# Attention: key tiles of row pitch 128, small tiles moved, so that all matmul operands share one byte residue modulo 256

## The chip, the core and the metric

The kernel runs on one NeuronCore of a Trainium2 chip. TensorE (PE in the profile) does the matrix products and the transposes; VectorE (DVE), ScalarE (ACT) and GpSimd (POOL) do the elementwise work; SyncE (SP) issues most DMAs. The metric is device time in microseconds (us) of one execution; the times given are medians of several runs.

In a matmul here the *stationary* operand is a 128x128 tile that is first loaded into the array (PEld in the profile), and the *moving* operand streams through it, 128x512 in most products of this kernel. Both lie in SBUF, 128 partitions with a line of bytes each; the result goes to PSUM. Where a tile begins in its line is decided by the order and the sizes in which pools and tiles are allocated. "Byte residue" below is that start address modulo 256.

## The reference, cut to what matters

One encoder layer over 2048 positions of width 1024: a projection, a gated linear attention (group A), a latent attention (group B), an output projection and a layer norm. The change lies in group B, a dense softmax attention with 4 heads over all 2048 keys:

```python
def attend(blk):
    qn, qr = blk
    s = (jnp.einsum('bqhd,bkhd->bhqk', qn, k_nope, preferred_element_type=jnp.float32)
         + jnp.einsum('bqhr,bkr->bhqk', qr, k_r, preferred_element_type=jnp.float32))
    p = jax.nn.softmax(s, axis=-1)
    return jnp.einsum('bhqk,bkhv->bqhv', p.astype(v.dtype), v)
...
x = layer_norm(DEEPNORM_ALPHA * x + mixed, ln_g[layer], ln_b[layer])
```

The kernel absorbs the up-projections into the queries and the output, so that all four heads share one key of width 128 (`ckvT`), one rotary key (`krs`) and one value (`vh`, `vl`).

## The kernel before

Every fp32 value that enters a matmul is split into a high part (rounded to fp32r, by ACT) and a low part (the rest, by DVE or POOL). A product is then three matmuls: high x high, high x low, low x high (`mm3`, lines 420 to 422).

The program has four stages. `sweep_a` (to about 380 us) projects x for group A, with weights `wah`, `wal` and products `ipa`; the gate's products `ipg` have the moving operand `wgh`/`wgl`, 512 wide, and the stationary `xah`/`xal`. `sweep_c` projects x for group B and fills the key and value tiles (`c_ckvTh`, `c_ckvTl`, `c_krT`, `vh`, `vl`), one row of 128 floats for each of 16 chunks of 128 positions. `attention` follows, and an output projection closes, with products `po`, `pmb`, `px` (moving `woh`/`wol`, 512 wide; stationary `oh`/`ol`); its first products run inside the last block of attention.

`attention` runs 16 blocks (4 heads x 4 groups of 512 queries). A block has 8 units of two key tiles. For each key tile `scores` issues five matmuls (lines 1521 to 1525) with a row of `ckvT_h`, `ckvT_l` or `krs` stationary and a query tile `qh`, `ql`, `rh`, `rl` moving, all 512 wide, into the PSUM tile `pS`. ACT copies `pS` to `s` (L1530), DVE keeps a running maximum `rm` (L1543). After the 8 units `tmax` transposes `rm` on PE (`mx`, L1549), `rmax` reduces it to a column `mc` (L1554), `bmax` transposes it back (`mb`, L1561). DVE subtracts (L1567), ACT takes the exponential (L1571), ACT and POOL split it into `ph` and `pl` (L366, L372), and `pv` multiplies: `ph` or `pl` moving, a row of `vh` or `vl` stationary, six matmuls for each unit, into `o`. The sums go through `tsum` (`sx`, L1630) to a column `rc` (`rcp`); `turn` and `rows` do that for the last block, with a row tile `rr` that is named `rt`. `y` is three more matmuls, with `ofh`, `ofl` moving.

A table of places (`PLACE` and its like) sorts all these steps into one order, and each engine runs its instructions in that order. So the scores of one block alternate with the value products of the block before.

The pools: `wz` holds the query tiles (and later `oh`, `ol`), `sp` the scores `s`, `bp` the tiles `ph`, `pl`, `ofh`, `ofl`, `wv_h`, `wv_l`, and, between them, the columns `mc` and `rc` and the row tile of `rows`. `smo` (of `OutProj`) holds small tiles of the output stage. `res`, on the right side, holds the three key tiles with `KW` = 132 floats (528 bytes) for a row of 128, and the two value tiles with 128. A tile `edge` of 32 bytes on the right side is never read or written.

Of the kernel before, what the change touches and what calls it, by code (L numbers as in the profile page):

```python
# [9 lines left out]
F32 = mybir.dt.float32  # L10
F32R = mybir.dt.float32r
# [7 lines left out]
P = 128  # L19
# [8 lines left out]
QB = 512  # L28
NQB = S // QB
NKT = S // P  # L30
KW = P + 4
TAU_INV = 1.0 / 16.0
RMS_EPS = 1e-6
LN_EPS = 1e-5
# [106 lines left out]
    tm=(0.532, 1.152),  # L141
# [79 lines left out]
    tm=(0.445, 1.143),  # L221
# [65 lines left out]
    tm=(0.495, 1.083),  # L287
# [68 lines left out]
class K:  # L356
# [141 lines left out]
    def run(self):  # L498
        tc, nc, ins = self.tc, self.nc, self.ins
        with ExitStack() as top:  # L500
            cp = top.enter_context(tc.tile_pool(name="const", bufs=1))
            self.cp = cp
            dp = top.enter_context(tc.tile_pool(name="scr", bufs=1, space=DRAM))
            self.qd_s = [dp.tile([P, H * P], F32, name=f"qd_s{c}") for c in range(NCH)]
            self.oi_s = [dp.tile([P, H * P], F32, name=f"oi_s{c}") for c in range(NCH)]
            self.su_s = [dp.tile([P, H * P], F32, name=f"su_s{c}") for c in range(NCH)]
            self.u_s = [dp.tile([P, H * P], F32, name=f"u_s{c}") for c in range(NCH)]
            self.qa_s = [[dp.tile([P, H, QB], F32, name=f"q{p}_s{b}") for p in "hl"] for b in range(NQB)]
            self.qr_s = [[dp.tile([H, 64, QB], F32, name=f"r{p}_s{b}") for p in "hl"] for b in range(NQB)]
            self.gm_s = [dp.tile([P, H, QB], F32, name=f"gm_s{b}") for b in range(NQB)]  # L510
            self.oa_s = [dp.tile([P, H, P], F32, name=f"oa_s{c}") for c in range(NCH)]
            self.r_s = [dp.tile([1, H, QB], F32, name=f"r_s{b}") for b in range(NQB)]
            self.ob_s = [dp.tile([P, H, QB], F32, name=f"ob_s{b}") for b in range(NQB)]

            ident = cp.tile([P, P], F32, name="ident")
            self.ident = ident
            self.gkv_c = cp.tile([P, 1], F32, name="gkv_c")
            self.gn_c = cp.tile([P, 1], F32, name="gn_c")
            self.cw = cp.tile([P, NCH, 3, H], F32, name="cw")

            psum = ExitStack()
            pspool = lambda n: psum.enter_context(tc.tile_pool(name=n, bufs=2, space=PSUM, reuse_waits="tile"))
            self.gp, self.ip, self.tr = pspool("gp"), pspool("ip"), pspool("tr")
            self.xfp = top.enter_context(tc.tile_pool(name="xfp", bufs=2, reuse_waits="tile"))
            edge = top.enter_context(tc.tile_pool(name="edge", bufs=1, side="right"))
            edge.tile([P, 8], F32, name="edge")
            self.keep = top.enter_context(tc.tile_pool(name="keep", bufs=1, side="right", reuse_waits="tile"))
            wgs = ExitStack()
            self.wgp = wgs.enter_context(tc.tile_pool(name="wgp", bufs=2 * NK + 1, side="right", reuse_waits="tile"))
            self.xab = wgs.enter_context(tc.tile_pool(name="xab", bufs=2, side="right"))  # L530
            self.wgate = []
            self.wl = None
            self.sweep_a()
            self.wz = top.enter_context(tc.tile_pool(name="wz", bufs=2 * NK + 1, reuse_waits="tile"))
            bcs = ExitStack()
            self.wm = bcs.enter_context(tc.tile_pool(name="wm", bufs=2 * NK + 1, reuse_waits="tile"))
            self.bc = bcs.enter_context(tc.tile_pool(name="bc", bufs=1, reuse_waits="tile"))
            self.wl = bcs.enter_context(tc.tile_pool(name="wl", bufs=2, reuse_waits="tile"))
            self.late_gates()
            wgs.close()  # L540
            rp = top.enter_context(tc.tile_pool(name="res", bufs=1, side="right", reuse_waits="tile"))
            self.ckvT_h = rp.tile([P, NKT, KW], F32R, name="ckvT_h")
            self.ckvT_l = rp.tile([P, NKT, KW], F32R, name="ckvT_l")
            self.kr = rp.tile([P, NKT, KW], F32R, name="krs")
            self.vh = rp.tile([P, NKT, P], F32R, name="vh")
            self.vl = rp.tile([P, NKT, P], F32R, name="vl")
            self.sweep_c()
            bcs.close()
            psum.close()
            self.wof = top.enter_context(tc.tile_pool(name="wof", bufs=PRE_W, side="right", reuse_waits="tile"))  # L550
            self.attention()
# [59 lines left out]
    def sweep_a(self):  # L611
        tc, nc, ins, cp = self.tc, self.nc, self.ins, self.cp
        with ExitStack() as ctx:
# [94 lines left out]
            for i in range(4, NCH):  # L708
# [12 lines left out]
                if i == 9:  # L721
                    self.rope_tables(hpi)
            i = NCH - 1
            run("q", i)
            run("k", i)
            run("av", i - 1)
# [598 lines left out]
        self.lo(s["cqT_l"][:, :, j], d["tm"][:, 0:2], s["cqT_h"][:, :, j])  # L1325

    def c_ckvTh(self, d):
        self.hi(self.ckvT_h[:, d["c"], :P], d["tm"][:, 2])

    def c_ckvTl(self, d):  # L1330
        self.lo(self.ckvT_l[:, d["c"], :P], d["tm"][:, 2], self.ckvT_h[:, d["c"], :P])

    def c_krT(self, d):
        self.hi(self.kr[:, d["c"], :P], d["tm"][:, 3])


    def c_pqr(self, d):
# [149 lines left out]
    def attention(self):  # L1487
# [4 lines left out]
        with ExitStack() as ctx:  # L1492
            qp = self.wz
            sp = ctx.enter_context(tc.tile_pool(name="sp", bufs=NP + 4, reuse_waits="tile"))
            bp = ctx.enter_context(tc.tile_pool(name="bp", bufs=2, reuse_waits="tile"))
# [17 lines left out]
            def scores(i, j):  # L1513


                d = stt[i]
                qh, ql, rh, rl = d["q"]
                ps = d["ps", j] = pS.tile([P, 2, QB], F32, tag="pS", name=f"pS{i}_{j}")
                for e in range(2):
                    kh, kl, kr = (t[:, 2 * j + e, :P] for t in (self.ckvT_h, self.ckvT_l, self.kr))  # L1520
                    mm(ps[:, e], kh, qh, start=True, stop=False)  # L1521
                    mm(ps[:, e], kh, ql, start=False, stop=False)  # L1522
                    mm(ps[:, e], kl, qh, start=False, stop=False)  # L1523
                    mm(ps[:, e], kr, rh, start=False, stop=False)  # L1524
                    mm(ps[:, e], kr, rl, start=False, stop=True)  # L1525
# [24 lines left out]

            def rmax(i):
                d = stt[i]
                d["mc"] = bp.tile([P, 4], F32, tag="mc", name=f"mc{i}")
                V.tensor_reduce(d["mc"], d["x"], AX.X, ALU.max)  # L1554

            def bmax(i):
# [75 lines left out]
            def rcp(i):  # L1632

                d = stt[i]
                rc = bp.tile([P, 4], F32, tag="rc", name=f"rc{i}")
                V.tensor_reduce(rc, d["x"], AX.X, ALU.add)
                V.reciprocal(rc, rc)
                d["rc"] = rc
# [11 lines left out]

            def rows(i):
                h, b = blocks[i]
                rr = bp.tile([4, P], F32, tag="rm", name=f"rt{i}", bufs=1)
                Ac.activation(rr, stt[i]["rt"], AF.Copy)
                nc.sync.dma_start(self.r_s[b][:, h].rearrange("o (e p) -> (o e) p", p=P), rr)

# [32 lines left out]
            op = OutProj(self, ctx, qp, bp, sp, pS, pM, pX, pO, pA)  # L1689
# [14 lines left out]
            for i in range(nb):  # L1704
                for j in range(NP):
                    t = NP * i + j
                    put(t, scores, i, j)
                    for n, f in (("copy", copy), ("max", smax), ("sub", sub), ("exp", exp), ("hi", phi), ("lo", plo),
                                 ("pv", pv), ("acc", acc)):
                        if n != "acc" or j != SUM_POOL[0] or i == nb - 1:  # L1710
                            put(t + at(n, i, j), f, i, j)
                put(NP * i + at("acc0", i), acc0, i)
                for n, f in (("tmax", tmax), ("rmax", rmax), ("bmax", bmax)) + {nb - 1: (), nb - 2: own_late}.get(i, own):
                    put(NP * i + NP - 1 + at(n, i), f, i)
                if i + 2 < nb:
                    put(NP * i + 4.05, fetch, i + 2)
# [70 lines left out]
            for c in range(4, NCH):  # L1787
                with fixed():
                    split(c + 2)
                    load(c + 4)  # L1790
                    if 4 < c < NCH - 1:
                        op.load_res(rest[c + 1])
                    op.product(rest[c])
                    op.finish(rest[c])
                with self.after(*last.values()), fixed():
                    if c == 4:
                        keep(nb - 2)
                    for f in {4: (tot, oh, ol), 5: (tsum, rcp), 7: (turn, y, rows, yc)}.get(c, ()):
                        f(nb - 1)
# [212 lines left out]
```

## Time and profile before

| | |
|---|---|
| median of 3 runs | 1317.59 us (1316.13 to 1318.52) |
| profiled execution: span, first to last instruction | 1311.9 us |
| PE busy in it | 1288.3 us, 98% |
| DVE / ACT / POOL busy | 958.5 / 812.5 / 784.6 us |
| granted TensorE clock | 0.998 of full |

The profile gives the span of its execution, not that execution's time as the runs are timed; the median lies 5.7 us above the span, which is what lies around the first and the last instruction. A sum that is made on the trace is made against 1311.9 us and carried to 1317.59 us. Durations of matmuls in the profile overlap: a matmul is shown for some 395 ns while the next starts some 230 ns after it. What a matmul costs is the distance from its start to the next one's start, which the timeline view gives to 10 ns.

### The profile page before, as it was taken

The page shows a single profiled execution, that of the slowest core. Times are in us where ns is not written, and L with a number is a line of the kernel's source. Part 1 is how long each engine was busy: PE and PEld are TensorE (multiplying, and loading weights), DVE is VectorE, ACT ScalarE, POOL GpSimd, SP SyncE. Part 2 cuts the span into 40 slices and gives each one's busy share as a digit, 9 for nine tenths or more (in the row PEclk, how much of TensorE's full clock was granted, in tenths as well). Part 3 has the DMA queues.
Part 4 walks back from the last instruction along what each step waited for, and adds up shares of the span by engine and source line. Part 5 has one row for each costly group of instructions (what it writes and reads, how often), then busy time and mean ns, then how long its engine had stood idle before and what let it go on. Part 6 is the DMA issues. An engine that isn't in the chain of part 4 may idle for free.

```text
span 1311.9 us, 19981 instructions
## 1 busy us (share of the span) xinstructions
PE 1288.3 (98%) x7081; PEld 1129.9 (86%) x7081; DVE 958.5 (73%) x1712; ACT 812.5 (62%) x1339; POOL 784.6 (60%) x494
## 2 busy tenths in 40 slices
PE   7999999999999999999999999999999999999997
PEld 7999999999989999999788888888888887888786
DVE  7967684655675455554888888888888888468998
ACT  6765656555575656564687787888888888511110
POOL 0143333232457666671388888889999999844441
PEclk9999999999999999999999999999999999999999
DMA  8131313122475555565301111112223210366663
GB/s 283 61 100 53 93 53 92 49 76 71 147 245 173 197 194 177 201 202 177 121 1 41 41 42 41 41 57 59 63 66 102 51 41 9 121 208 174 210 195 121
DMA packets 107819, 145.81 MB, mean 111 GB/s; under 512 B 17250, under 2 KB 62694, under 8 KB 107720
## 3 DMA queue, kind: packets, MB, share of 16 engines
q1 hardware_dynamic: 99128, 142.41, 35.0%
q0 software_dynamic: 672, 2.10, 0.4%
q8 instruction: 56, 0.92, 0.3%
q10 hardware_dynamic: 7920, 0.03, 0.3%
q14 instruction: 43, 0.35, 0.2%
HBM read 94.14 MB, written 50.36 MB: 110 GB/s over the span
## 4 chain that ended last, share of the span: by engine, by line
PE 83%; DVE 4%; DMA 3%; ACT 2%; issue 2%; POOL 1%; SPq 1%; DVEq 0%; POOLq 0%; ACTq 0%
PE o L420 4%; PE o L421 4%; PE pS L1521 4%; PE pS L1524 4%; PE o L422 4%; PE pS L1523 4%; PE pS L1525 4%; PE pS L1522 4%; PE ipa L420 4%; PE ipa L422 4%; PE ipa L421 4%; PE pz L421 2%; PE pz L420 2%; PE pz L422 2%; PE ipg L420 2%; PE ipg L421 2%
## 5 line engine op out<-in xcount | busy, mean ns | idle before, releaser
L372 POOL TENSOR_TENSOR pl<-s,ph 128x1024 fp32r<-128x1024 f32 x128 | 306.9, 2412 | 66.7 <-ACT ph L366 61.5
L1543 DVE TENSOR_TENSOR rm<-pS,rm 128x512 f32<-128x512 f32 x210 | 144.8, 690 | 44.1 <-ACT s L1530 39.0
L1530 ACT ACTIVATE s<-pS 128x1024 f32<-128x1024 f32 x128 | 131.2, 1025 | 67.6 <-PE pS L1525 65.6
L1567 DVE TENSOR_TENSOR s<-s,mb 128x1024 f32<-128x1024 f32 x128 | 151.2, 1213 | 9.5 <-PE mb L1561 9.3
L1030 POOL TENSOR_TENSOR Us<-Us,cw 128x512 f32<-128x512 f32 x16 | 18.5, 1157 | 227.0 <-DVE Us L1028 175.2
L366 ACT ACTIVATE ph<-s 128x1024 fp32r<-128x1024 f32 x128 | 135.0, 1057 | 18.1 <-PE o L422 17.6
L1571 ACT ACTIVATE s<-s 128x1024 f32<-128x1024 f32 x128 | 131.4, 1050 | 13.8 <-DVE s L1567 13.7
L420 PE MATMUL ipa<-wah,xah 128*128 128x384 f32 (+1 forms) x384 | 130.6, 340 | 6.8 <-ACT wah L366 6.8
L422 PE MATMUL ipa<-wah,xal 128*128 128x384 f32 (+1 forms) x384 | 125.2, 326 | 0.0
L421 PE MATMUL ipa<-wal,xah 128*128 128x384 f32 (+1 forms) x384 | 125.0, 325 | 0.0
L1521 PE MATMUL pS<-qh,ckvT_h 128*128 128x512 f32 x256 | 103.7, 405 | 0.7 <-ACT s L1571 0.4
L420 PE MATMUL o<-ph,vh 128*128 128x512 f32 x256 | 102.6, 401 | 0.0
L422 PE MATMUL o<-ph,vl 128*128 128x512 f32 x256 | 101.3, 396 | 0.0
L1524 PE MATMUL pS<-rh,krs 128*128 128x512 f32 x256 | 101.2, 395 | 0.0
L421 PE MATMUL o<-pl,vh 128*128 128x512 f32 x256 | 101.1, 395 | 0.0
L1523 PE MATMUL pS<-qh,ckvT_l 128*128 128x512 f32 x256 | 100.9, 394 | 0.0
L1525 PE MATMUL pS<-rl,krs 128*128 128x512 f32 x256 | 100.7, 393 | 0.0
L1522 PE MATMUL pS<-ql,ckvT_h 128*128 128x512 f32 x256 | 100.6, 393 | 0.0
L1594 DVE TENSOR_TENSOR ap<-ap,s 128x512 f32<-128x512 f32 x120 | 83.1, 693 | 2.7 <-ACT s L1571 0.8
L372 POOL TENSOR_TENSOR ol<-of,oh 128x512 fp32r<-128x512 f32 x32 | 43.0, 1346 | 65.6 <-ACT oh L366 65.6
L420 PEld LDWEIGHTS ipa<-wah,xah 128*128 128x128 f32 x384 | 73.5, 192 | 7.6 <-ACT wah L366 6.8
L420 PE MATMUL pz<-xch,wzh 128*128 128x256 f32 x256 | 74.8, 292 | 0.0
(325 smaller groups left out, 3856.4 us busy)
## 6 DMA issues: line engine op xcount, KB each, us to landing
xcf<-xT_dram SPq DMA_DIRECT2D x16, 512.0 KB, 4.7
xr<-x_dram SPq DMA_DIRECT2D x16, 512.0 KB, 6.5
out_dram<-rr SPq DMA_DIRECT2D x32, 256.0 KB, 2.0
xaf<-xT_dram SPq DMA_DIRECT2D x14, 512.0 KB, 4.2
oib<-oi_s SPq DMA_DIRECT2D x16, 256.0 KB, 4.1
qdb<-qd_s SPq DMA_DIRECT2D x16, 256.0 KB, 4.6
SU<-su_s SPq DMA_DIRECT2D x16, 256.0 KB, 4.4
ub<-u_s SPq DMA_DIRECT2D x16, 256.0 KB, 4.7
```

What stands on the lines that cost most here:

```text
L366: return nc.scalar.activation(dst, src, AF.Copy).ins
L372: return e.tensor_tensor(dst, src, hi.bitcast(F32), ALU.subtract).ins
L420: mm(out, ah, bh, start=start, stop=False)
L421: mm(out, ah, bl, start=False, stop=False)
L422: mm(out, al, bh, start=False, stop=stop)
L1521: mm(ps[:, e], kh, qh, start=True, stop=False)
L1522: mm(ps[:, e], kh, ql, start=False, stop=False)
L1523: mm(ps[:, e], kl, qh, start=False, stop=False)
L1524: mm(ps[:, e], kr, rh, start=False, stop=False)
L1525: mm(ps[:, e], kr, rl, start=False, stop=True)
L1543: V.tensor_tensor(d["rm"], src[:, e], d["rm"], ALU.max)
L1567: V.tensor_tensor(s, s, d["mb"][:, None, :].to_broadcast([P, 2, QB]), ALU.subtract)
```

## The change

The key tiles get a row pitch of 128 floats (512 bytes), like the value tiles, and the columns `mc` and `rc` and the row tile `rr` move from the pool `bp` to `smo`. No arithmetic changes.

```diff
-KW = P + 4
...
-            self.ckvT_h = rp.tile([P, NKT, KW], F32R, name="ckvT_h")
-            self.ckvT_l = rp.tile([P, NKT, KW], F32R, name="ckvT_l")
-            self.kr = rp.tile([P, NKT, KW], F32R, name="krs")
+            self.ckvT_h = rp.tile([P, NKT, P], F32R, name="ckvT_h")
+            self.ckvT_l = rp.tile([P, NKT, P], F32R, name="ckvT_l")
+            self.kr = rp.tile([P, NKT, P], F32R, name="krs")
...
-        self.hi(self.ckvT_h[:, d["c"], :P], d["tm"][:, 2])
+        self.hi(self.ckvT_h[:, d["c"]], d["tm"][:, 2])
...
-                    kh, kl, kr = (t[:, 2 * j + e, :P] for t in (self.ckvT_h, self.ckvT_l, self.kr))
+                    kh, kl, kr = (t[:, 2 * j + e] for t in (self.ckvT_h, self.ckvT_l, self.kr))
...
-                d["mc"] = bp.tile([P, 4], F32, tag="mc", name=f"mc{i}")
+                d["mc"] = op.sm.tile([P, 4], F32, tag="mc", name=f"mc{i}")
...
-                rc = bp.tile([P, 4], F32, tag="rc", name=f"rc{i}")
+                rc = op.sm.tile([P, 4], F32, tag="rc", name=f"rc{i}")
...
-                rr = bp.tile([4, P], F32, tag="rm", name=f"rt{i}", bufs=1)
+                rr = op.sm.tile([4, P], F32, tag="rm", name=f"rt{i}", bufs=1)
```

What that does to the places, from the addresses in the two built programs (bytes modulo 256, of every tile or row that stands):

| operand | role | before | with the change |
|---|---|---|---|
| `qh`, `ql`, `rh`, `rl` | moving, scores | 192 | 192 |
| rows of `ckvT_h`, `ckvT_l`, `krs`, key tile kt | stationary, scores | 192 + 16 kt, modulo 256 | 192 |
| `ph`, `pl` | moving, products with the values | 0 | 192 |
| rows of `vh`, `vl` | stationary | 192 | 192 |
| `ofh` / `ofl` | moving, `y` | 0 / 192 | 192 / 192 |
| `wv_h`, `wv_l` | stationary, `y` | 192 | 192 |
| `ident` | moving, transposes | 128 | 128 |
| `wgh`, `wgl` and `xah`, `xal` | gate in `sweep_a` | 192 and 192 | 192 and 192 |
| `woh`, `wol` and `oh`, `ol` | output projection | 192 and 192 | 192 and 192 |
| `wmh`, `wml` and `xch`, `xcl` | `ipm` in `sweep_c`, 448 wide | 192 and 192 | 192 and 192 |

The order of the instructions is the same on all five engines. What moves is one group of waits. `mc` now lies where an `oT` tile of `sweep_c` lay, so the first `mc` must wait for the DMAs that stored it; before, the first `rc` lay there and waited. On DVE, at the first maximum of attention (`rm` running maximum, `mx` the transposed maximum in PSUM), before:

```order
L1543 TENSOR_TENSOR rm_7865<-s_6_7952,rm_7865 128x512 [waits DVE_49]
L1543 TENSOR_TENSOR rm_7865<-s_7_7967,rm_7865 128x512 [waits DVE_49,Activation_49]
L1543 TENSOR_TENSOR rm_7865<-s_7_7967,rm_7865 128x512 [waits DVE_49]
L1554 TENSOR_REDUCE mc_7987<-mx_7982 128x4 [waits PE_49]
L1540 TENSOR_TENSOR rm_8007<-pS_0_7969,s_0_7994 128x512 [waits DVE_49,Activation_49]
L1567 TENSOR_TENSOR s_2_7882<-s_2_7882,mb_7989 128x1024 [waits PE_49]
```

and with the change:

```order
L1542 TENSOR_TENSOR rm_7865<-s_6_7952,rm_7865 128x512 [waits DVE_49]
L1542 TENSOR_TENSOR rm_7865<-s_7_7967,rm_7865 128x512 [waits DVE_49,Activation_49]
L1542 TENSOR_TENSOR rm_7865<-s_7_7967,rm_7865 128x512 [waits DVE_49]
L1553 TENSOR_REDUCE mc_7987<-mx_7982 128x4 [waits DMAHW5_49,DMAHW3_49,DMAHW7_49,DMAHW1_49,PE_49]
L1539 TENSOR_TENSOR rm_8007<-pS_0_7969,s_0_7994 128x512 [waits DVE_49,Activation_49]
L1566 TENSOR_TENSOR s_2_7882<-s_2_7882,mb_7989 128x1024 [waits PE_49]
```

The four DMA waits stand ahead of the first `mc`, and in exchange the first `rc`, a block later, waits for PE alone. Every line number above 31 is one lower.

More of the change, by code (lines that the diff above doesn't have):

```diff
@@ L1327, in c_ckvTh @@
     def c_ckvTh(self, d):
-        self.hi(self.ckvT_h[:, d["c"], :P], d["tm"][:, 2])
+        self.hi(self.ckvT_h[:, d["c"]], d["tm"][:, 2])
     def c_ckvTl(self, d):
-        self.lo(self.ckvT_l[:, d["c"], :P], d["tm"][:, 2], self.ckvT_h[:, d["c"], :P])
+        self.lo(self.ckvT_l[:, d["c"]], d["tm"][:, 2], self.ckvT_h[:, d["c"]])
     def c_krT(self, d):
-        self.hi(self.kr[:, d["c"], :P], d["tm"][:, 3])
+        self.hi(self.kr[:, d["c"]], d["tm"][:, 3])
     def c_pqr(self, d):
```

## The prediction

> **What bounds the kernel now.** I read the chain of waits first, then the busy times by stage, then PE's timeline, start by start.
>
> ```profile
> PE 83%; DVE 4%; DMA 3%; ACT 2%; issue 2%; POOL 1%; SPq 1%; DVEq 0%; POOLq 0%; ACTq 0%
> 0.00:616.40 616.40, 603.98 (x4000) 571.88 (x4001) 382.05 (x901) 373.05 (x830) 267.95 (x248) 1.00 0.44 138
> 616.40:1159.40 543.00, 540.56 (x2427) 438.61 (x2426) 441.41 (x589) 418.00 (x450) 453.12 (x198) 1.00 0.21 59
> 1159.40:1311.90 152.50, 143.78 (x658) 119.39 (x657) 135.02 (x224) 21.47 (x59) 63.49 (x48) 0.98 0.60 189
> 794.03 0.44 PE mb L1561 x4
> 825.77 0.44 PE mb L1561 x4
> 857.51 0.44 PE mb L1561 x4
> ...
> 1107.91 0.63 PE mx L1549 x4
> ...
> 1151.38 3.44 DMA xr<-x_dram
> ```
>
> The first row is the chain's shares by engine. In the next three each engine has its busy time and its count: PE, PEld, DVE, ACT, POOL; the second of them is attention, where PE is busy 540.56 of 543.00 us. The rest are pieces of the chain. The three `mb`, one for each block, have PE work alone between them, 31.74 us apart both times; the last block's maximum follows at 1107.91, and at 1151.38 the chain leaves PE for a load. So in attention a block lasts as long as PE's matmuls need, and the question is what one costs.
>
> ```profile
> 792.04 0.60 PE L1549 MATMUL mx<-ident,rm 128*128 128x128 f32 x4
> 792.40 0.48 PE L420 MATMUL o<-ph,vh 128*128 128x512 f32 x1
> 792.72 0.40 PE L421 MATMUL o<-pl,vh 128*128 128x512 f32 x1
> ```
>
> Four transposes take 0.36 us to the next start, and the 512-wide matmul behind them 0.32. A block has three such sets (`mx`, `mb`, `sx`), 2.04 us, and 128 other 512-wide matmuls (80 scores, 48 with the values, 3 of `y`, less the three just counted). They get (31.74 - 2.04)/128 = 232.0 ns each. The clock is 1.00 here, so it isn't the throttle.
>
> **The same shape elsewhere is cheaper.** The output projection streams 128x512 too:
>
> ```profile
> 1192.36 0.60 PE L1630 MATMUL sx<-ident,acc 128*128 128x128 f32 x4
> 1192.71 0.48 PE L420 MATMUL pmb<-woh,oh 128*128 128x512 f32 x1
> 1193.03 0.40 PE L421 MATMUL pmb<-wol,oh 128*128 128x512 f32 x1
> 1194.19 0.40 PE L420 MATMUL pmb<-woh,oh 128*128 128x512 f32 x1
> 1195.57 0.39 PE L420 MATMUL pmb<-woh,oh 128*128 128x512 f32 x1
> 1214.38 0.39 PE L422 MATMUL po<-woh,ol 128*128 128x512 f32 x1
> 1195.57:1214.38 18.81, 18.81 (x84) 15.58 (x83) 12.11 (x21) 2.19 (x5) 10.15 (x8) 1.00 0.63 169
> ```
>
> From 1195.57 to 1214.38 there are 84 starts, 83 distances: 226.6 ns. Right behind the transposes it is slower: 5 distances from 1193.03 to 1194.19 (232 ns), 11 to 1195.57 (230.9). So a stream whose operands all have residue 192 settles at 226.6 within eleven matmuls of a disturbance, which costs 11 x 4.3 = 47 ns, or 5 x 5.4 = 27 if it is cut off after five.
>
> Is it the residue, or is it that ACT has little to do there? Two stretches tell these apart.
>
> ```profile
> 79.74 0.39 PE L420 MATMUL ipg<-wgh,xah 128*128 128x512 f32 x1
> 84.27 0.39 PE L422 MATMUL ipg<-wgh,xal 128*128 128x512 f32 x1
> 79.74:84.27 4.53, 4.53 (x21) 3.75 (x20) 4.17 (x4) 0.61 (x2) 3.23 (x2) 1.00 0.14 33
> 1133.49 0.40 PE L420 MATMUL po<-woh,oh 128*128 128x512 f32 x1
> 1136.26 0.40 PE L420 MATMUL o<-ph,vh 128*128 128x512 f32 x1
> 789.72 0.39 PE L1521 MATMUL pS<-qh,ckvT_h 128*128 128x512 f32 x1
> 790.87 0.40 PE L1521 MATMUL pS<-qh,ckvT_h 128*128 128x512 f32 x1
> ```
>
> The gate's products in `sweep_a`, residue 192 throughout, take 4.53/20 = 226.5 ns with DVE and POOL busy. The output projection's own products, put in twelves between products with `ph` and `pl` (residue 0) in the last block, take 2.77/12 = 230.8. So the price follows the operands and what ran just before, not the stage. The last two rows are the case against: the five scores of key tile 0 have residue 192 on both sides already, and take 1.15/5 = 230 ns. I read them as the eleven-long settling seen above, cut off after five; but it is a reading.
>
> **The change part by part.**
>
> *Scores and value products.* All 131 matmuls of a block come to residue 192 on both sides. Of a steady block: three sets 2.04, 128 x 226.6 = 29.00, settling 27 ns behind `mx` (its six matmuls end in `mb`) and 47 behind `mb` and `sx`, 0.12. Sum 31.16, so 0.58 us less. Blocks 2 to 14 are thirteen of them: 7.5 us. The last block's part to 1107 us has the same matmuls: 0.55. From there to the end of its products at 1159 the mix of `o` and `po` runs at 230.8 or less, some with its settling already in it: of the 170 or so to 1151, where DMAs and DVE take the chain over, at most 0.7; I take 0.5.
>
> ```profile
> 616.40:635.10 18.70, 18.70 (x84) 15.17 (x83) 11.25 (x16) 9.73 (x11) 1.30 (x1) 1.00 0.82 261
> 635.10:662.70 27.60, 25.79 (x113) 20.10 (x112) 23.77 (x31) 22.11 (x24) 16.23 (x7) 1.00 0.10 29
> ```
>
> Block 0 is 80 scores with PE full: 80 x 5.4 less one settling, 0.4. In block 1 PE idles 1.8 us for DVE and ACT, so its gain is between nothing and 0.5; I take 0.1, since what waits ends on the others. Sum: 7.5 + 0.55 + 0.5 + 0.4 + 0.1 = 9.05 us.
>
> Bounds: at best no settling is lost and all of blocks 1 and 15 counts, 13 x 128 x 5.4 = 9.0, and 0.7 + 0.7 + 0.43 + 0.5: 11.3 us. At least, if the stream settles only half of the time between its disturbances, half of 9.05: 4.5 us.
>
> The Trainium skill speaks against any gain: on the page "TensorE: Matmul & The Clock Gate", section "Step-by-step: what each phase is for", it says that loading the next tile's weights "doesn't steal SBUF read bandwidth from the running matmul", the two having ports of their own. By it an address can't matter, and the time stays. The 226.6, 230.8 and 232.0 ns of one shape at one clock don't fit it.
>
> *Do the others follow?* A block 0.58 us shorter needs data 0.58 us sooner.
>
> ```profile
> 792.68 0.69 DVE L1554 TENSOR_REDUCE mc<-mx 128x4 f32<-128x512 f32 x1 [0.96 <-PE mx L1549]
> 793.87 0.60 PE L1561 MATMUL mb<-ident,mc 128*128 128x128 f32 x4
> 1043.60:1075.40 31.80, 31.80 (x145) 25.84 (x144) 27.06 (x37) 26.41 (x30) 31.27 (x16) 1.00 0.17 41
> 1045.58 7.14 POOL L372 TENSOR_TENSOR pl<-s,ph 128x1024 fp32r<-128x1024 f32 x3
> 1055.90 0.40 PE L421 MATMUL o<-pl,vh 128*128 128x512 f32 x1
> ```
>
> The tightest hand-over of a steady block is `mc`: it ends at 793.37, 0.50 us ahead of the transposes that read it, and only six matmuls (0.03 us of gain) lie between the maximum's transposes and these. POOL is the engine to watch: in block 14 it works 31.27 us, more than the 31.16 that the block would last. But the third `pl` of the group ends at 1052.72, 3.18 us before PE takes it, so POOL may fall behind by 0.1 to 0.5 us in each of three blocks without a wait.
>
> *The moved wait.*
>
> ```profile
> 618.14 0.58 SPq L1458 DMA_DIRECT2D oa_s<-oT  x1
> DMA to landing us min/median/max: 2.0/4.0/10.1
> 638.50 0.69 DVE L1554 TENSOR_REDUCE mc<-mx 128x4 f32<-128x512 f32 x1 [0.75 <-PE mx L1549]
> ```
>
> The last store of an `oT` is issued at 618.14 and the slowest of them lands after 10.1 us, so by 628.3; the first `mc` starts at 638.50. Behind it on DVE stand block 1's maximum and the subtractions, which PE waits for; with ten us of cover the price is nothing, and it would be the lateness of the store otherwise. The other small tiles move without a wait. `ph` and `pl` are written at another residue by ACT and POOL; POOL's `pl` takes 7.14/3 = 2.38 us at residue 0, and I expect the same.
>
> The output stage has the operands that it had. It starts 9 us sooner and lasts as long.
>
> **Rivals.** *The residue does nothing* (attention's own traffic makes the 232). For it: key tile 0. Against: `po` at 230.8 and 226.6. Time 1317.6. It is what the skill's rule above would give.
>
> *Slower: a shared residue settles at a dearer distance.* A stream need not settle low:
>
> ```profile
> 463.12 0.37 PE L422 MATMUL ipm<-wmh,xcl 128*128 128x448 f32 x1
> 466.22 0.36 PE L422 MATMUL ipm<-wmh,xcl 128*128 128x448 f32 x1
> ```
>
> These 448-wide products have residue 192 everywhere and stand at 3.10/15 = 206.7 ns, 0.461 ns a column. At that rate a 512-wide one takes 236.2, 4.2 more than now: 4.2 x 128 x 15 = 8.1 us, 1325.7. It decides from 232.0 on. Against it: width and pitch of the changed operands are those of the output projection, not of `ipm`.
>
> *POOL becomes the bound* from block 13 on: the gain there (three blocks, 1.7 us) is lost, and as much again if the output stage's splits, which POOL makes in the same blocks, come late: 9.05 - 3.4 = 5.7, 1311.9. Against it stand the 3.18 us above.
>
> **How the numbers follow.** Forecast 0.80, time 1317.59 - 9.05 = 1308.5 us. POOL 0.06, no effect 0.09, slower 0.05. A measurement of this kernel tells some 0.2% from no change, 2.6 us: forecast and POOL are faster (0.86), no effect is the same (0.09), the rest slower (0.05). The range goes from the upper bound, 1317.6 - 11.3 = 1306.3, to the lower, 1317.6 - 4.5 = 1313.1, and holds the POOL case; it leaves out the 0.14 of the last two and little more.
>
> **What would show it.** The block's period between two `mb` in the chain: 31.16, not 31.74. PE's starts in a long run of scores and value products: 226 to 227 ns from the twelfth behind a set of transposes, about 231 before it. PE busy without a gap in blocks 2 to 14. The stage before 616 us unchanged, and the output stage as long as now. It would be wrong if the period stays at 31.74 (residue without effect), if it shrinks but gaps with a POOL or DVE releaser appear, or if the scores settle while the value products do not (then a score or a value product has another cause, and only one of 80 to 48 parts of the gain comes).

## The result, and the profile after

| | time, median us (lowest to highest) | ratio to before, 95% interval |
|---|---|---|
| before | 1316.86 (1314.53 to 1318.52), 6 runs | |
| with the change | 1307.47 (1306.02 to 1310.94), 6 runs | 0.9937 (0.9926 to 0.9947) |
| both once more, on another occasion | 1315.19 and 1305.86 | 0.9933 (0.9921 to 0.9946) |

The forecast was 1308.5 us with a range from 1306.3 to 1313.1. The profiled execution of the changed kernel took 1308.66 us by its own time, with a span of 1306.3: some 2.4 us lie around a span, not the 5.7 that the part on the time before supposed. The profiled execution of before was thus one of its shorter ones. The sum of the prediction is not touched by it, since it is a difference. The two medians of six runs lie 9.4 us apart, and the ratio of 0.9937 stands for 8.3 us; the forecast was 9.05.

The chain's shares by engine, then three windows of the changed kernel: up to attention, attention to its last product with the values, and the rest. The columns are those shown of before.

```profile
PE 83%; DMA 4%; DVE 3%; ACT 2%; POOL 1%; issue 1%; SPq 1%; DVEq 0%; POOLq 0%; ACTq 0%
```

```profile
0.00:616.55 616.55, 605.06 (x4000) 572.77 (x4001) 381.89 (x901) 373.34 (x830) 267.96 (x248) 1.00 0.44 138
616.55:1150.00 533.45, 530.54 (x2427) 437.60 (x2426) 441.19 (x589) 417.87 (x450) 452.26 (x198) 1.00 0.22 60
1150.00:1306.30 156.30, 145.31 (x658) 120.51 (x656) 135.17 (x224) 21.59 (x59) 63.41 (x48) 0.97 0.60 185
```

The first stage is as long as before (616.55 against 616.40 us). Attention has the same 2427 matmuls and lasts 533.45 instead of 543.00 us: the whole gain is there. The output stage lasts 156.30 instead of 152.50 us, and its granted clock is 0.97 instead of 0.98: 3.8 us are given back there in this execution.

PE's timeline in block 6, start by start:

```profile
791.04 0.60 PE L1560 MATMUL mb<-ident,mc 128*128 128x128 f32 x4
791.40 0.48 PE L1520 MATMUL pS<-qh,ckvT_h 128*128 128x512 f32 x1
791.71 0.40 PE L1521 MATMUL pS<-ql,ckvT_h 128*128 128x512 f32 x1
793.80 0.39 PE L419 MATMUL o<-ph,vh 128*128 128x512 f32 x1
801.28 0.39 PE L1520 MATMUL pS<-qh,ckvT_h 128*128 128x512 f32 x1
822.16 0.60 PE L1560 MATMUL mb<-ident,mc 128*128 128x128 f32 x4
853.25 0.60 PE L1560 MATMUL mb<-ident,mc 128*128 128x128 f32 x4
```

From one `mb` to the next it is 31.12 and 31.09 us (31.74 before). Behind the transposes the stream is still unsettled: nine distances from 791.71 to 793.80, 232 ns each. From 793.80 to 801.28, through value products and scores alike, 33 distances take 226.7 ns each. Settled runs of both kinds have one price, and it is that of the output projection.

What is new stands in the output stage:

```profile
1185.22 14.26 DMA gr<-gm_s
1199.50 0.92 SPq L1853
1200.46 7.79 DMA xr<-x_dram
1208.38 0.70 DVE rr L1926
```

```profile
1205.67 0.40 PE L421 MATMUL y<-ofh,wv_l 128*128 128x512 f32 x1
1209.22 0.47 PE L419 MATMUL pmb<-woh,oh 128*128 128x512 f32 x1 [3.15 <-DVE rr L1926]
1209.82 0.63 PE L421 MATMUL pmb<-woh,ol 128*128 128x512 f32 x1
1212.81 0.53 PE L419 MATMUL pmb<-woh,oh 128*128 128x512 f32 x1
```

```profile
1209.80:1213.00 3.20, 3.20 (x9) 2.50 (x8) 3.10 (x7) 0.92 (x3) 0.39 (x1) 0.50 0.76 235
```

The first fence is from the chain, the second from PE's timeline, the third a window. Behind the last `y` PE stands still: DVE's residual `rr` waits for the load `xr`, which SP issues at 1200.46, behind four loads of `of` and `gr`. From `y` to the next start it is 3.55 us; before, at the same place, it is 1.34:

```profile
1215.17 0.40 PE L422 MATMUL y<-ofh,wv_l 128*128 128x512 f32 x1
1216.51 0.47 PE L420 MATMUL pmb<-woh,oh 128*128 128x512 f32 x1 [0.94 <-DVE rr L1927]
```

In the changed kernel's window behind that stall the granted clock is 0.50, and the seven distances from 1209.82 to 1212.81 are 427 ns each, 200 more than those of the matmuls that follow: 1.4 us.

### The profile page after: what moved, and what is told of

Read it like the earlier page. It is cut to its first block, busy times and chain, and to the rows that moved or that the text cites. A ratio compares the mean times of both kernels' runs of the same rounds, so it can differ in the third digit from the quotient of the medians.

```text
span 1306.3 us, 19979 instructions
## 1 busy us (share of the span) xinstructions
PE 1280.9 (98%) x7081; PEld 1130.9 (87%) x7081; DVE 958.2 (73%) x1712; ACT 812.8 (62%) x1339; POOL 783.6 (60%) x494
## 4 chain that ended last, share of the span: by engine, by line
PE 83%; DMA 4%; DVE 3%; ACT 2%; POOL 1%; issue 1%; SPq 1%; DVEq 0%; POOLq 0%; ACTq 0%
PE pS L1520 4%; PE o L419 4%; PE o L420 4%; PE o L421 4%; PE pS L1522 4%; PE pS L1523 4%; PE pS L1521 4%; PE pS L1524 4%; PE ipa L419 4%; PE ipa L421 4%; PE ipa L420 4%; PE pz L420 2%; PE pz L419 2%; PE pz L421 2%; PE ipg L419 2%; PE ipg L420 2%
## 5 line engine op out<-in xcount | busy, mean ns | idle before, releaser
L1529 ACT ACTIVATE s<-pS 128x1024 f32<-128x1024 f32 x128 | 131.4, 1027 | 60.6 <-PE pS L1524 51.3
```

## The experiments

The first ones test what sets the price of a matmul: its own two operands, or the run in which it stands; and whether equal residues are needed or a regular pitch is enough.

**One half of the change each.** The key tiles alone:

```diff
-KW = P + 4
+KW = P
```

> The kernel before with the key tiles at a pitch of 128 floats, so that all scores have residue 192 on both sides; mc, rc and rr stay in bp, so that ph and pl stay at residue 0. Theory (a stream settles at 226.6 ns only when a long run of it has one residue, and any matmul of two residues unsettles it): scores run in tens between six value products, so neither settles in a steady block. Scores stay at 230 to 231 ns, value products at 232, the period at 31.6 to 31.7 us (31.74 before, 31.10 with the whole change), and the time falls by 0 to 2 us, ratio 0.9985 to 1.000. Block 0, which has scores alone, does settle: 226 to 227 ns. Rival (each matmul's price is set by its own two residues): the 80 scores of a block take 226.6 each, the value products 232: period 31.74 - 80 x 0.0054 = 31.3 us, time 6 us less, ratio 0.995.

and on the kernel before, the small tiles alone:

```diff
-                d["mc"] = bp.tile([P, 4], F32, tag="mc", name=f"mc{i}")
+                d["mc"] = op.sm.tile([P, 4], F32, tag="mc", name=f"mc{i}")
...
-                rc = bp.tile([P, 4], F32, tag="rc", name=f"rc{i}")
+                rc = op.sm.tile([P, 4], F32, tag="rc", name=f"rc{i}")
...
-                rr = bp.tile([4, P], F32, tag="rm", name=f"rt{i}", bufs=1)
+                rr = op.sm.tile([4, P], F32, tag="rm", name=f"rt{i}", bufs=1)
```

> The kernel before with mc, rc and rr in smo, so that ph and pl come to residue 192 like vh and vl; the key tiles keep the pitch of 132 floats. Theory (one residue over a long run): value products run in sixes between scores of unequal residues and do not settle: 231 ns or more, the scores 232, the period 31.6 to 31.74 us, ratio 0.9985 to 1.000. Block 0 as before, 232 ns. Rival (each matmul by its own residues): 48 value products of a block at 226.6: period 31.74 - 48 x 0.0054 = 31.48 us, time 3.9 us less, ratio 0.997. The two halves then add up to the whole; by the theory they do not.

Measured: keys alone 1311.67 us, ratio 0.9976 (0.9965 to 0.9987); small tiles alone 1311.39, ratio 0.9969 (0.9958 to 0.9980). The means are over all 512-wide matmuls of blocks 2 to 13, without the one right behind a set of transposes:

| | period, us | scores, ns | value products, ns |
|---|---|---|---|
| before | 31.74 | 232.1 | 232.5 |
| keys alone | 31.50 | 229.9 | 230.6 |
| small tiles alone | 31.51 | 231.6 | 228.7 |
| both | 31.10 | 227.3 | 227.3 |

On the period both expectations miss. The halves bring 0.24 and 0.23 us of a period, the whole 0.64: they do not add up, so the price is not set by a matmul's own operands (that rule gave 31.3 for the keys). But they bring more than the theory left them (0 to 0.1). PE's timeline of the keys alone shows why:

```profile
799.10 0.40 PE L420 MATMUL o<-ph,vh 128*128 128x512 f32 x1
801.87 0.40 PE L1521 MATMUL pS<-qh,ckvT_h 128*128 128x512 f32 x1
804.19 0.60 PE L1630 MATMUL sx<-ident,acc 128*128 128x128 f32 x4
805.77 0.39 PE L1521 MATMUL pS<-qh,ckvT_h 128*128 128x512 f32 x1
806.91 0.40 PE L420 MATMUL o<-ph,vh 128*128 128x512 f32 x1
```

Ten scores, all of residue 192 on both sides, that follow twelve value products of two residues take 2.32 us, 232 ns each; the five from 805.77, which follow other scores, take 1.13 to 1.14 us, 227 each. And the twelve value products from 799.10 to 801.87, whose operands are as before, take 230 to 231 (before, the mean of all was 232.5). So a matmul's price depends on what ran before it, as the theory says; a stream with two kinds of operands settles in parts of each run, which the theory had denied.

On block 0, which has scores alone, both expectations hold. With the keys alone, from the eighth score on:

```profile
617.94 0.39 PE L1523 MATMUL pS<-qh,ckvT_l 128*128 128x512 f32 x1
631.99 0.39 PE L1525 MATMUL pS<-rl,krs 128*128 128x512 f32 x1
```

These are 62 distances of 226.6 ns. With the small tiles alone, where the scores keep their unequal residues, the distances of block 0, all but the first, lie between 225 and 238 ns, 232 in the mean, as before.

**A constant difference.** In the changed kernel the key and value tiles are moved as a whole, pitch and order kept:

```diff
+            rp.tile([P, 16], F32, name="pad1")
             self.ckvT_h = rp.tile([P, NKT, P], F32R, name="ckvT_h")
...
             self.vl = rp.tile([P, NKT, P], F32R, name="vl")
+            rp.tile([P, 48], F32, name="pad2")
```

> The changed kernel with the key and value tiles moved by 64 bytes as a whole: stationary operands at residue 0 in every score and value product, moving ones at 192. The pitch is regular, the small tiles are moved, but the two residues differ, always by the same amount. Theory (the two residues must be equal): scores and value products do not settle, 231 to 233 ns, period 31.6 to 31.8 us, ratio 0.998 to 1.000. Rival (one regular pitch, the same address pattern from matmul to matmul, is what counts, or the moved small tiles): 226 to 227 ns, period 31.1 us, ratio 0.994 as with the change. The output projection, which is not touched, stays at 226.6 ns in either case.

Three more of the kind, with 32 and 32 floats, 8 and 56, 64 and 64:

> The changed kernel with the key and value tiles moved by 128 bytes: stationary operands at residue 64, moving ones at 192, in all scores and value products. Theory (equal modulo 256 is needed): a uniform stream settles at the price seen with 64 bytes between them, 233.3 ns, period 31.87 us. Rival (equal modulo 128 is enough): 226.7 ns and 31.10 us, as with the change.

> The changed kernel with the key and value tiles moved by 32 bytes: stationary operands at residue 224, moving ones at 192. Theory (the two must be equal to the byte): 233.3 ns, period 31.87 us. Rival (only the line of 64 bytes in which both lie counts, 192 to 255): 226.7 ns, 31.10 us.

> The changed kernel with the key and value tiles moved by 256 bytes: residues equal modulo 256, not modulo 512 (in the changed kernel they are equal modulo 512 as well). Theory (modulo 256, as the change has it): 226.7 ns, period 31.10 us. Rival (equal modulo 512 is needed): 233 ns, 31.85 us, as with 32, 64 and 128 bytes between them.

| stationary ahead of moving by | period, us | mean of 512-wide, ns | time, us |
|---|---|---|---|
| 0 (the change) | 31.10 | 227.3 | 1307.47 |
| 32 bytes | 31.85 | 233.1 | 1317.33, one run |
| 64 bytes | 31.86 | 233.2 | 1316.94, ratio 1.0016 (1.0007 to 1.0024) |
| 128 bytes | 31.84 | 233.1 | 1318.07, one run |
| 256 bytes | 31.13 | 227.5 | 1306.91, one run |

PE's timelines: 64 bytes ahead, then 32, then 256, each with the first and the last start of a run of scores and value products that no transposes break:

```profile
809.65 0.39 PE L419 MATMUL o<-ph,vh 128*128 128x512 f32 x1
817.82 0.39 PE L1524 MATMUL pS<-qh,ckvT_l 128*128 128x512 f32 x1
```

```profile
809.04 0.40 PE L1522 MATMUL pS<-qh,ckvT_h 128*128 128x512 f32 x1
817.67 0.40 PE L1522 MATMUL pS<-qh,ckvT_h 128*128 128x512 f32 x1
```

```profile
808.29 0.39 PE L419 MATMUL o<-ph,vh 128*128 128x512 f32 x1
814.41 0.39 PE L1522 MATMUL pS<-qh,ckvT_h 128*128 128x512 f32 x1
```

The runs are 35, 37 and 27 distances long: 233.4, 233.2 and 226.7 ns. So a regular pitch is worth nothing without equal residues. The first expectation had such a stream not settle, at 231 to 233 ns; it does settle, but at a dearer distance, a little above the mixture of before (232.2 ns), and with 64 bytes the kernel is slower than before with an interval above 1. A difference of 32 bytes, with both operands in the same stretch of 64, is enough to lose the gain, and so is one of 128; one of 256 loses nothing. So for these products the change's "modulo 256" is borne out from both sides. What was moved here, the key and value tiles, is read by PE alone during attention, which points to PE's own reads. The moved small tiles are in all these kernels: where they lie is no cause of its own.

**Another common residue.** All that is allocated after `sweep_a` is shifted, so that scores, value products and output projection have residue 0 on both sides:

```diff
+            top.enter_context(tc.tile_pool(name="shift", bufs=1)).tile([P, 16], F32, name="pad1")
             self.wz = top.enter_context(tc.tile_pool(name="wz", bufs=2 * NK + 1, reuse_waits="tile"))
...
             self.vl = rp.tile([P, NKT, P], F32R, name="vl")
+            rp.tile([P, 48], F32, name="pad2")
```

> The changed kernel with everything that is allocated after sweep_a moved by 64 bytes or as much modulo 256 on both sides: queries, ph, pl, keys, values, weights of the output projection all at residue 0. Theory (what counts is that the two residues are equal): 226.7 ns, period 31.10 us, output projection 226.6 ns as now. Rival (residue 192 itself is the good one): 232 to 233.3 ns, period 31.7 to 31.9 us, output projection slower too.

```profile
806.79 0.39 PE L419 MATMUL o<-ph,vh 128*128 128x512 f32 x1
816.54 0.39 PE L1522 MATMUL pS<-qh,ckvT_h 128*128 128x512 f32 x1
```

43 distances of 226.7 ns, period 31.17 us, 1307.90 us in one run; the output projection stands at 226.7. The 0.07 us by which the period exceeds the change's lie in the settling (mean of all 227.8 ns, not 227.3). Equality counts, not the value 192.

**The transposes.** `ident` at 192:

```diff
+            cp.tile([P, 16], F32, name="pad1")
             ident = cp.tile([P, P], F32, name="ident")
+            cp.tile([P, 48], F32, name="pad2")
```

> The changed kernel with ident at residue 192 in place of 128, so that the transposes too have one residue (mx and sx on both sides; mb has it in the first of its four columns). Theory (a residue that differs unsettles the stream): the matmuls behind a set of transposes stand at 226.7 ns from the second on, and the period falls by what settling costs now, 128 x (227.26 - 226.67) = 0.08 us, to 31.02. Rival (any matmul of another shape unsettles it): 224 to 236 ns for the first ten as now, period 31.10 us.

The period stays at 31.10, and the first matmuls behind a set still go from 224 to 236 ns. The rival holds: a matmul of another shape unsettles the stream, with the identity at 192 as at 128. (The one time, 1304.11 us, is an execution whose attention began 1.6 us sooner and whose output stage kept its clock; the period says that it isn't the edit.)

**Another stage.** Equal residues in `sweep_a`'s projection, which the change leaves unequal although the title says "all", by a row of 1088 floats:

```diff
+A_AT = (0, 320, 704)
...
-            wa = [[wp.tile([P, NA], F32R, name=f"wa{p}{k}") for p in "hl"] for k in range(NK)]
+            wa = [[wp.tile([P, 1088], F32R, name=f"wa{p}{k}") for p in "hl"] for k in range(NK)]
...
-            wh, wl = self.wa[k]
-            self.mm3(pt[:, :n], xh[:, k, 0], xl[:, k, 0], wh[:, c0:c0 + n], wl[:, c0:c0 + n],
+            wh, wl = (t[:, A_AT[g]:A_AT[g] + n] for t in self.wa[k])
+            self.mm3(pt[:, :n], xh[:, k, 0], xl[:, k, 0], wh, wl,
```

(the splits that write the tiles go to the same places).

> The changed kernel, and in sweep_a the weight tiles wah, wal get a row of 1088 floats with their three column groups at 0, 320 and 704, so that all operands of ipa have residue 192 (now wah 64 and wal 192 in the 384-wide groups, wal 64 in the 288-wide one). Theory (equal residue is cheaper in general, not in attention alone): the 384-wide products with wah fall from 177.9 and 176.3 ns to the 173 of those with wal, the 288-wide ones stay at 132: 256 x 4.9 + 256 x 3.3 ns = 2.1 us off sweep_a, if PE sets its pace there; ratio 0.992. Rival (what helped is peculiar to attention): ipa prices as they are, ratio 0.9937 as with the change alone.

Measured: 1309.46 us, ratio 0.9953 (0.9939 to 0.9967), no better than the change alone. The next stage begins at 372.29 us, and at 371.8 to 374.0 in the profiles of the other kernels here, so no gain in `sweep_a` is clear of that spread. The 384-wide products stand at 174.7, 174.3 and 175.5 ns (`wah` with `xah`, `wal` with `xah`, `wah` with `xal`) instead of 177.9, 172.8 and 176.3: levelled, but in the mean only 0.8 ns cheaper, since the ones that had equal residues get dearer. Where such a run has settled, each takes 173.3 ns; but a run is 24 long. The theory's 2.1 us took 172.8 for the price of an equal pair, and that was the same mistake as pricing a matmul by its own operands. Two rows of this kernel's PE, one of its DVE, then DVE's row of the changed kernel show what came later:

```profile
385.58 0.28 PE L422 MATMUL pz<-xch,wzl 128*128 128x256 f32 x1
387.11 0.38 PE L1417 MATMUL Ob<-MMb,qhb 128*128 128x256 f32 x1 [1.24 <-POOL MMb L372]
```

```profile
373.59 8.96 DVE L372 TENSOR_TENSOR wzl<-wzr,wzh 128x512 fp32r<-128x512 f32 x8
```

```profile
374.84 5.97 DVE L371 TENSOR_TENSOR wzl<-wzr,wzh 128x512 fp32r<-128x512 f32 x8
```

The splits of `wzl` take 8.96 instead of 5.97 us on DVE, while POOL works on `Sf` beside them (sooner here, since its load came sooner); PE waits for `wzl` and `MMb`, and behind these waits its granted clock is 0.91 from 382 to 400 us (1.00 in the changed kernel). Attention starts at 619.58 instead of 616.57. That the two engines hold each other up is read from this one profile and was not tried by itself.

**The stall in the output stage.** In the changed kernel:

```diff
                     split(c + 2)
-                    load(c + 4)
                     if 4 < c < NCH - 1:
                         op.load_res(rest[c + 1])
+                    load(c + 4)
```

> The changed kernel; in the output stage the load of the next chunk's xr is issued ahead of the four loads of the chunk three further on, and not behind them. Theory (xr, held up in SP's queue behind loads that wait, is what PE waits for after the last y): xr is issued about 8 us sooner, the stall is gone but for 0.6 us or less, no matmul runs at half the clock, and the time falls by 2 to 3.5 us more: ratio to before 0.991 to 0.992. Rival (PE waits for something else there, DVE's residual or the turn of the last block): stall and time as with the change, ratio 0.9937.

the changed kernel beside it, and the same edit in the kernel before:

> The changed kernel once more, beside the two that load xr sooner. Theory (the output stage gives back part of the gain: PE waits 2 to 3.5 us behind the last y for xr, and where it waits longer than about 2.2 us the next eight or so matmuls run at half the clock): ratio to before 0.993 to 0.9945, and a stall of over 2 us behind the last y. Rival (the 3545 ns stall of the first profile was a chance of that execution): a stall of about 1.3 us, as in the profile of before.

> The kernel before with only the load of xr moved ahead. Theory (the same stall stands there with 1.3 us): 1 to 1.5 us less, ratio 0.999; the change's own gain on top of it is then what attention gained, 9.4 us, ratio of the two with xr first 0.993. Rival: nothing, ratio 1.000.

| | without | with `xr` first |
|---|---|---|
| before | 1315.19 | 1312.98, ratio 0.9989 (0.9980 to 0.9998) |
| with the change | 1305.86 (1304.03 to 1306.15), ratio 0.9933 (0.9921 to 0.9946) | 1303.17 (1302.20 to 1303.83), ratio 0.9913 (0.9898 to 0.9928) |

SP's and PE's rows of the changed kernel with `xr` first:

```profile
1191.47 0.46 SPq L1872 DMA_DIRECT2D xr<-x_dram  x1
1194.42 2.25 SPq L1850 DMA_DIRECT2D of<-oa_s  x1
```

```profile
1205.82 0.40 PE L421 MATMUL y<-ofh,wv_l 128*128 128x512 f32 x1
1206.05 0.39 PE L419 MATMUL pmb<-woh,oh 128*128 128x512 f32 x1
```

`xr` is issued nine us sooner and PE goes on after 0.23 us; no distance of 0.43 us follows. The edit brings 2.7 us on the change (the two ranges of runs do not overlap), and on the kernel before 1.4 us by the ratio, 2.2 by the medians, where the theory had 1.0 to 1.5. In the changed kernel the stall varies from execution to execution; it was 3.55 us in the first profile, and in the one taken here:

```profile
1206.11 0.40 PE L421 MATMUL y<-ofh,wv_l 128*128 128x512 f32 x1
1207.99 0.47 PE L419 MATMUL pmb<-woh,oh 128*128 128x512 f32 x1 [1.48 <-DVE rr L1926]
```

That is 1.88 us, less than the 2 that was expected, with no slow clock behind it, and the output stage is 153.0 us long. With `xr` first in both, the change is worth 1312.98 - 1303.17 = 9.8 us. This version, 1303.17 us, beats both kernels.

## Why the prediction was right, point by point

| term, us | predicted | first profile | second profile |
|---|---|---|---|
| blocks 2 to 14 | 7.5 | 8.27 | 8.27 |
| last block to its maximum | 0.55 | 0.32 | 0.31 |
| from there to the last value product | 0.5 | 0.61 | 0.63 |
| block 0 | 0.4 | 0.06 | 0.40 |
| block 1 | 0.1 | 0.31 | 0.30 |
| sum | 9.05 | 9.57 | 9.91 |
| output stage | 0 | -3.8 | -0.5 |

The steady blocks, which carry the forecast, came out as the mechanism had it, 8.27 us for 7.5. That the time came out at 1307.5 us, only 1.0 from the forecast, is in part luck: attention gave 0.5 to 0.9 us more than forecast, and the output stage, put at nothing, took 0.5 to 3.8 back.

*What bounds it.* PE sets attention's pace before and after; in blocks 2 to 14 no PE gap appeared in either profile, so a cheaper matmul is a shorter block.

*Is it the residue?* Shown for these 512-wide products. The differences of 32, 64 and 128 bytes lose the gain, 256 bytes and a common residue of 0 keep it. The five scores of key tile 0, which had equal residues and still took 230 ns, were read as a settling cut off; the keys-alone kernel shows ten such scores at 232 ns behind value products of two residues. That reading holds.

*The steady block.* Forecast 31.16, measured 31.10. The step that was off is the settling, put at 27 + 47 + 47 = 121 ns a block from one row of the output projection. Over blocks 2 to 13 of the first profile, what the 512-wide matmuls take above 226.67 ns, counted up to the next set, is 30 ns behind `mx`, 12 or 50 behind `mb` in turn (hence 31.09 and 31.12), and 15 behind `sx`: 76 in the mean. Behind `mb` the stream stands after nine distances or after three, behind `sx` after three. The three sets with the matmul behind each take 2.01 us, not 2.04. These two terms make up, to 0.01 us, the 0.06 us a block between 31.16 and 31.10, and thirteen times that is the difference between 7.5 and 8.27.

*Blocks 0 and 1.* Block 1 gave 0.3, inside the 0 to 0.5 that the forecast left it; block 0 gave its 0.40 in one execution and next to nothing in the other, where PE stood still near its end for ACT's copy `s` (L1529), a wait that the forecast had only for block 1.

*The last block.* It gave 0.32 us up to its maximum, not 0.55: ahead of its `mx`, PE idles for 0.97 us where it idled for 0.63, both times for DVE's running maximum `rm`.

*Do the others follow?* They did, with little to spare. A window of block 14, and POOL's `pl` in it:

```profile
1035.76:1066.88 31.12, 31.12 (x144) 25.75 (x143) 27.00 (x36) 26.37 (x30) 31.04 (x15) 1.00 0.18 43
```

```profile
1038.01 7.14 POOL L371 TENSOR_TENSOR pl<-s,ph 128x1024 fp32r<-128x1024 f32 x3
```

POOL is busy 31.04 of 31.12 us there, and its three `pl` take the 7.14 us that they took before. The rival of a POOL bound did not come about, but the next gain in a block of that kind would meet it.

*The moved wait.* `mc` of block 0 starts 0.69 us after the start of its transposes, before (637.81 to 638.50) and after:

```profile
637.90 0.66 PE L1548 MATMUL mx<-ident,rm 128*128 128x128 f32 x4 [0.31 <-DVE rm L1542]
```

```profile
638.59 0.69 DVE L1553 TENSOR_REDUCE mc<-mx 128x4 f32<-128x512 f32 x1 [0.75 <-DMA rh<-rh_s]
```

DVE's row names a load in place of the transposes, but the wait is as long as before: nothing was late.

*The output stage.* "It starts 9 us sooner and lasts as long" is the sentence that failed in the first profile. The operands are the same and the matmuls too, but its loads wait in one queue behind stores and behind slots that come free, and a stall there was in the profile of before already (1.34 us). It was not priced, and the clock behind it neither.

*The rivals.* No effect is ruled out by the difference of 64 bytes, with 233.4 ns against 226.7 for the same matmuls in the same order: where the weights lie matters to the stream. The Trainium skill, page "TensorE: Matmul & The Clock Gate", section "Step-by-step: what each phase is for", says that loading the next weights takes no read bandwidth from the running matmul. The two distances do not fit that. What the two reads share was not found out here. The rival of a dearer settled distance is what a constant difference does; equal residues do not, at a width of 512. But its row, the 448-wide `ipm` at 206.7 ns with residue 192 on both sides, is not explained: no run here tried it, and equal residues are thus not shown to be enough at every width.

## What to carry to other kernels

In long streams of 512-wide fp32r matmuls with a new stationary tile each time, see to it that moving and stationary operands begin at the same byte modulo 256: pad rows and small tiles by that, and change all streams that alternate, since one of them alone keeps the others unsettled. At other widths measure first. Where runs are short and broken by other shapes (the 384-wide products here), the gain is smaller (0.8 of 175.7 ns, against 5.0 of 232.2) and easily lost to what moves behind it. After any gain on the bounding engine look at the next stage's loads: what is queued behind loads that wait for their buffers will stop it there.

## What the runs showed of the hardware

A stream of 128x512 matmuls, each with new weights, has settled distances: 226.7 ns where the two operands' residues are equal modulo 256, some 233.3 where they differ by 32 or 64 bytes. It remembers a break for four to ten matmuls. If at a granted clock of 0.50 a column takes one period, the 427 ns that 512 columns took there make a period of the full clock 0.417 ns. By that estimate the two distances are 544 and 560 periods, 32 and 48 above the 512 columns; why it is these numbers stays open.

A pause of PE is followed by matmuls at half the clock sometimes. The changed kernel moved by 256 bytes:

```profile
1205.13 0.40 PE L421 MATMUL y<-ofh,wv_l 128*128 128x512 f32 x1
1207.50 0.47 PE L419 MATMUL pmb<-woh,oh 128*128 128x512 f32 x1 [1.97 <-DVE rr L1928]
1209.03 0.63 PE L421 MATMUL pmb<-woh,ol 128*128 128x512 f32 x1
1209.45 0.63 PE L419 MATMUL pmb<-woh,oh 128*128 128x512 f32 x1
```

and the one with `ident` at 192:

```profile
1203.55 0.40 PE L421 MATMUL y<-ofh,wv_l 128*128 128x512 f32 x1
1206.29 0.47 PE L419 MATMUL pmb<-woh,oh 128*128 128x512 f32 x1 [2.35 <-DVE rr L1928]
1206.83 0.39 PE L421 MATMUL pmb<-woh,ol 128*128 128x512 f32 x1
1207.06 0.39 PE L419 MATMUL pmb<-woh,oh 128*128 128x512 f32 x1
```

An idle time of 1.97 us was followed by the slow clock, one of 2.35 us was not. Over the profiles of all the kernels here, the pause behind the last `y`, start to start, was followed by distances of 427 ns after 2.23, 2.37, 2.66, 2.81 and 3.55 us, and not after 2.25, 2.38, 2.54 and 2.74 us, nor after 2.02 us or less; so the 2.2 us that an expectation above supposed is no threshold. The Trainium skill, page "TensorE: Matmul & The Clock Gate", section "Why this matters for your kernels", advises against PE idle gaps above some 3 us, and its section "What's actually happening" has a free-running window of 3.4 us behind it. That pauses of one length end in either way would fit a window that runs freely. That 1.97 us of idle time were enough does not fit one that has to be idle throughout, and the figure of 3 us is too kind.
